# Rewriting a mixer's vector work and order, and starting each SwiGLU stage with three units on the first token half

## The chip, the cores and the metric

The kernel runs on one core of a Trainium2 chip. The metric is the device time of one execution in microseconds (us). Each engine (TensorE for matmuls, VectorE, ScalarE, GpSimd, and SyncE, which issues the DMAs) runs its own instructions in its own fixed order and waits for others by semaphores.

## What is computed

One inference step of a two-layer encoder for 64 sample tokens and 512 prompt tokens, 576 in all, in float32. Per layer, cut to what matters:

```
x = x + 0.5 * post1(SwiGLU_1(pre1(x)))            # w_gate, w_up: 1024 x 2816, w_down: 2816 x 1024
h = pre2(x); z = h @ w_in[l]                      # q_a 384, kv_a 256, kpe 64, hq hf hi hg 256 each, cu cv 256 each
mix = concat[MLA(512) | HGRN2(256) | chunk-gMLP(256)] @ w_out[l]
x = x + post2(mix)
x = x + 0.5 * post3(SwiGLU_2(pre3(x)))
# HGRN2, chunks of 64:  A[t,s] = sum_e q[t,e] k[s,e] exp(b[t,e] - b[s,e]) for s <= t;  o = A v + (q exp b) S
#   o = rmsnorm per head (o, out_g) * silu(hg)
# chunk-gMLP: u = gelu(cu); v = rmsnorm per group (gelu(cv), v_g); out = u * (tril(w_s) v + b_s)
# MLA: c = rmsnorm(kv_a, g) joins the cached latents, the rotary key joins the cached keys; softmax attention
```

All norms are RMS norms over a row. The outputs are y for both groups, and per layer the new latents, rotary keys, HGRN states and gMLP rows.

## The kernel before

**Tiling.** Tokens lie in the free dimension, in two halves of 288 columns (`HALF`); features lie in 8 blocks of 128 partitions. A matmul in float32 is three matmuls of rounded parts (`three`): hi x hi, hi x lo, lo x hi. A weight chunk (`cols`, L121 to L130) is loaded raw by SyncE, then ScalarE writes its rounded part `wh` (L126) and VectorE the remainder `wl` (L127). A unit of gate or up, u, is 8 feature blocks x 3 matmuls for each half.

**Stages.** Six stages run: FFN(0,0), mixer 0, FFN(0,1), FFN(1,0), mixer 1, FFN(1,1), named by layer and place. Each ends by making its update d of the token stream x: per half, `after` spawns `post`, in which the column sum `ss` of squares (an accumulation by L315, then TensorE) gives m (L236), its root p comes from GpSimd (L151) and is spread over partitions by flips (`bc`, transposes on TensorE, L73); then for each feature block d is scaled (L253), added to x (L256) and split into hh and hl (L142); GpSimd sums the squares for the next norm (L198), and `pre_stats` (ss, m L209, root rn, bc) gives the factor `rbc` of the next stage. Here L198 stands for acc, L240 for p.

**FFN.** `ffn` (L327) begins with four weight chunks (`self.ahead`, from `first`, L274): gate and up of the feature blocks f = 0 and 1, prepared while the stage before ends. It runs them on half 0 as soon as x of half 0 is there (`together` waits in the plan for `pre_done`), then on half 1; f = 2 and 3 follow as units on both halves. `evac` (L335 to L341) multiplies by rbc, takes Silu and multiplies. The blocks f = 4 to 21 follow in pairs (`seven`), then `d` by w_down in groups, whose last one ends with three tail blocks half by half.

**Mixer.** `mixer` (L1046) projects by columns of w_in: hq and hf first, then natural rows (tokens in partitions) of hi and hg (vg), cu and cv (uv), then kv_a and kpe in 320 columns (tile n), then three units of q_a (u). Generators run beside it. `hgrn` (L650) makes the decay products: 14 items of a level h and one of two key blocks m. `make` (L695) writes e by two subtractions (L701, L702) and Exp (L703), the product w = k * e on GpSimd (L705), and zb = q * e on VectorE (L711, two per item); `use` multiplies them on TensorE (lv, ls) and copies by a mask (L726, L733). Then come states (su), outputs (o, `out`, L839 and L841), gMLP rows (`cmlp`, L851 to L870) and the normalised latents cn (`latent`, L902), each flipped on TensorE (tp) through one of two small PSUM buffers. `caches` brings the cached latents (ck, cch) and `rotary_key` the rotary key (kd, kp); then v, q, k and the attention.

**What sets the order.** `Net` is a planner: it adds up an estimated TensorE time `self.t` for each matmul, and a spawned generator is stepped when its planned time has come (`spawn`, `tick`, `until`); a `yield` says how long to wait for the next step. `self.pace` (L59) is the planned time between two decay items. The engines' rows are afterwards put in order by a scheduler, by priority and readiness; `keep_in_program_order` pins chosen instructions.

Of the kernel before, what the change touches and what calls it, by code (L numbers as in the profile page):

```python
# [49 lines left out]
class Net:  # L50
    def __init__(self, tc, i, o):
        self.tc = tc
        self.nc = tc.nc
        self.i = i
        self.o = o
        self.count = 0
        self.bg = []
        self.t = 0.0
        self.pace, self.apace, self.l1, self.l2, self.l3 = 3.0, 2.16, 1.26, 3.94, 2.15  # L59

# [266 lines left out]
    def ffn(self, l, j, gpost, gpre, gain, nxt, packed):  # L327
# [14 lines left out]

        chs, self.ahead = self.ahead, None
        for hf in (0, 1):
            o = self.units(chs, hf, 2 if gpost is self.g0 else 4)
            if hf == 0:
                self.until(lambda: 0 in self.stats_done)
                for f in (0, 1):
                    evac(f, 0, o[2 * f][0], o[2 * f + 1][0])
        chs = None  # L350
        ops = self.combine(gain)
        self.until(lambda: 1 in self.stats_done)
        for f in (0, 1):
            evac(f, 1, o[2 * f][1], o[2 * f + 1][1])
        o = None
        for f in (2, 3):
            pg = self.unit(self.cols(wg, f * P))
            pu = self.unit(self.cols(wu, f * P))
            for hf in (0, 1):
                evac(f, hf, pg[hf], pu[hf])  # L360
        for f in range(4, NF, 2):
# [5 lines left out]
        for a, (g0, g1) in enumerate(GROUPS):  # L367
# [36 lines left out]
            if last:  # L404
                chs = [self.cols(wd, m * P, P, g0, g1 - g0) for m in range(tail, KT)]
                self.ahead = [self.cols(*q) for q in nxt]
                for hf in (0, 1):
                    for m in range(tail, KT):
                        run(m, chs[m - tail], [hf])
                    self.after(hf, d, acc, gpost, gpre, (r, r2), packed)  # L410

# [213 lines left out]
    def group_norm(self, src):  # L625
        nc = self.nc
        sq = self.slot("gsq")
        nc.scalar.activation(sq[:, :256], src, AF.Square)
        ss = self.small("gs", 4)
        nc.vector.tensor_reduce(ss, sq[:, :256].rearrange("p (g d) -> p g d", g=4), AX.X, ALU.add)  # L630
        nc.vector.tensor_scalar(ss, ss, 1.0 / 64, EPS, op0=ALU.mult, op1=ALU.add)
        r = self.small("gr", 4)
        self.rsqrt(r, ss, 4)
        return r.unsqueeze(2).to_broadcast([P, 4, 64])

    def to_mix(self, src, k0, i):
        ps = self.sm("tp")
        for e in range(2):
            self.flip(ps[:, e * P:(e + 1) * P], src[:, e * P:(e + 1) * P])
        c, w = tcol(i), twid(i)  # L640
        for e in range(2):
            self.split(self.mixh[k0 + e][:, c:c + w], self.mixl[k0 + e][:, c:c + w], ps[:, e * P:e * P + w])

# [6 lines left out]
    def hgrn(self, l, zq, zf, vg):  # L650
# [36 lines left out]
        for m in range(2):  # L687
            qk.append(self.slot("qk"))
            nc.gpsimd.tensor_tensor(qk[m], q[m], kk[m], op=ALU.mult)
        items = [(li, h, m) for li, h in enumerate(LEVELS) for m in range(2)]  # L690
        ready = {}

        def make(n):
# [18 lines left out]
            ready[n] = (w, z)  # L712

# [59 lines left out]
        for m in range(2):  # L773
            e = self.slot("e")
            nc.vector.tensor_tensor(e[:, :64], b[m][:, 63:64].to_broadcast([P, 64]), b[m][:, :64], op=ALU.subtract)
            bv = b[m][:, 64:].rearrange("p (b x) -> p b x", x=P)
            nc.vector.tensor_tensor(e[:, 64:].rearrange("p (b x) -> p b x", x=P),
                                    bv[:, :, P - 1:P].to_broadcast([P, 4, P]), bv, op=ALU.subtract)
            nc.scalar.activation(e, e, AF.Exp)
            eb[m] = self.slot("eb")  # L780
            nc.scalar.activation(eb[m], b[m], AF.Exp)
            nc.gpsimd.tensor_tensor(e, e, kk[m], op=ALU.mult)
# [18 lines left out]
        for i in (1, 2, 3, 4, 0):  # L801
            for m in range(2):
# [7 lines left out]
                for g in range(2):  # L810
# [8 lines left out]
                yield 0.1  # L819
        while not self.gated:  # L820
# [3 lines left out]
        def out(i):  # L824
# [14 lines left out]
            nc.vector.tensor_tensor(on[:, :256].rearrange("p (g d) -> p g d", g=4),  # L839
                                    ps[:, :256].rearrange("p (g d) -> p g d", g=4), r, op=ALU.mult)  # L840
            nc.vector.tensor_tensor(on[:, :256], on[:, :256], vg[i][:, 256:512], op=ALU.mult)  # L841
            yield 7.71
            self.to_mix(on, 4, i)
            self.left -= 1
# [6 lines left out]
    def cmlp(self, l, i, t, c):  # L851
        nc = self.nc
        v = t[:, 256:512]
        r = self.group_norm(v)
        vv = v.rearrange("p (g d) -> p g d", g=4)
# [21 lines left out]
    def gates(self, l, c, vg, uv):  # L877
# [3 lines left out]
        for i in range(5):  # L881
            nc.scalar.activation(uv[i][:, :512], uv[i][:, :512], AF.Gelu_apprx_tanh)
            self.spawn(self.cmlp(l, i, uv[i], c), 0.8 + 2.59 * i)
        for i in range(5):
            g = vg[i][:, 256:512]
            nc.scalar.activation(g, g, AF.Silu)
            nc.gpsimd.tensor_tensor(g, g, c["og"], op=ALU.mult)
        self.gated = True


    def latent(self, l, i, ps, c, r, kr, cth, ctl):
# [13 lines left out]
        else:  # L905
            nc.sync.dma_start(self.o["ckv_p"][l, 0, (i - 1) * P:i * P], cn[:, :256])
        yield 4.0
        if not cth:
# [137 lines left out]
    def mixer(self, l, gpost, gpre, nxt, packed):  # L1046
# [14 lines left out]

        c["og"] = self.gain_rows("hgrn_out_g", l)
        nch = self.nat_chunks(w, 1216, 512)
# [149 lines left out]
        for k0 in (4, 0):  # L1213
# [29 lines left out]
            if k0 == 0:  # L1243
                for m in range(tail, KT, 2):
                    chs[m // 2] = self.cols(wo, m * P, 2 * P, k0, 4)
                self.ahead = [self.cols(*q) for q in nxt]
                for hf in (0, 1):
                    for m in range(tail, KT):
                        run(m, [hf])
                    self.after(hf, d, acc, gpost, gpre, None, packed)  # L1250

# [33 lines left out]
    def bounds(self, more):  # L1285
        nc = self.nc
        ps = self.sm("tp")
        self.flip(ps[:, :18], more)
        nc.vector.tensor_copy(self.colg[:, 96:], ps[:, :18])

# [18 lines left out]
    def build(self):  # L1309
# [9 lines left out]

        pin = tc.keep_in_program_order  # L1320
        self.ident = load("ident", [P, P])
# [23 lines left out]
        for _ in range(8):  # L1345
            self.mul(self.warm[:, :P], self.ones, self.ones, True, True)
        self.colg = const.tile([P, 114], F32, name="colg", tag="colg")
        ps = self.sm("tp")
# [27 lines left out]
        load_x(4)  # L1376
        self.ahead += [self.cols(*q) for q in todo[2:]]
        more = const.tile([18, P], F32, name="more", tag="more")
        nc.sync.dma_start(more[0:6], i["mla_qa_g"].rearrange("l (k p) -> (l k) p", p=P))
        nc.sync.dma_start(more[6:10], i["hgrn_lb_logits"].rearrange("l (k p) -> (l k) p", p=P))  # L1380
        nc.sync.dma_start(more[10:18], i["cmlp_b_s"].rearrange("l g t -> (l g) t"))
        self.bs = self.colg[:, 106:114]
        self.spawn(self.pre_stats(0, 0.17, sums))
        self.spawn(start(1), 4.06)
# [77 lines left out]
```

## Time and profile before

| | us |
|---|---|
| median of 3 runs | 2287.99 |
| lowest, highest | 2287.04, 2290.99 |
| profiled execution | 2284.6 |
| its span | 2282.8 |
| TensorE busy | 2214.3 (97%) |
| VectorE busy | 1554.9 (68%) |
| ScalarE busy | 1093.4 (48%) |
| GpSimd busy | 225.6 (10%) |

The span runs from the first to the last instruction; the time of the execution has what lies around it as well. Busy time of TensorE counts matmuls at whichever clock was granted. The mixers lie at about 431 to 731 and 1557 to 1860 us; the FFN stages fill the rest.

### The profile page before, as it was taken

Reading aid. Unit: us, or ns where it says so; the run is one execution under the profiler, and the core shown is the slowest. Engines: PE = TensorE matmul, PEld = TensorE weight load, DVE = VectorE, ACT = ScalarE, POOL = GpSimd, SP = SyncE. Lnnn points to the kernel's source line nnn. Section 1 sums busy time; section 2 is a strip of 40 time slices with the busy share of each in tenths; the row PEclk is TensorE's granted clock in tenths of the full one; section 3 lists DMA queues with packets and bytes.
Section 4 is the critical chain, followed back from the end, with each engine's and each line's share of the span. In section 5 each row is a group of like instructions: output and inputs, shape, how many; then the busy total and the mean of one; then the engine's idle time right before and its main releaser. Section 6 shows DMA issues by size and latency. Waiting matters only on the chain.

```text
span 2282.8 us, 39582 instructions
## 1 busy us (share of the span) xinstructions
PE 2214.3 (97%) x15988; PEld 2157.1 (94%) x15988; DVE 1554.9 (68%) x2627; ACT 1093.4 (48%) x1917; POOL 225.6 (10%) x230
## 2 busy tenths in 40 slices
PE   9999999998899999999999999999988999999998
PEld 8999999888799999999999999998887999999998
DVE  6787643787666888845597875447975678887443
ACT  7444442466554644443354444324645645444423
POOL 0000000343301100000020000004332020000000
PEclk9999999999999999999999999999999999999999
DMA  7333442312112333344133334423121232333421
GB/s 218 93 93 93 120 135 84 98 53 78 54 57 79 107 93 93 94 129 125 56 98 93 93 89 133 127 65 102 40 87 48 63 112 72 98 93 101 122 70 42
DMA packets 339531, 211.06 MB, mean 92 GB/s; under 512 B 17378, under 2 KB 319700, under 8 KB 339348
## 3 DMA queue, kind: packets, MB, share of 16 engines
q1 hardware_dynamic: 339348, 208.54, 30.6%
q8 instruction: 125, 2.05, 0.4%
q14 instruction: 58, 0.48, 0.1%
HBM read 190.11 MB, written 18.38 MB: 91 GB/s over the span
## 4 chain that ended last, share of the span: by engine, by line
PE 80%; DVE 10%; ACT 3%; issue 3%; POOL 3%; DMA 0%; SPq 0%; POOLq 0%; DVEq 0%; ACTq 0%
PE d L68 24%; PE X L68 20%; PE Q L68 10%; PE u L68 8%; PE R L68 5%; PE wo L68 4%; DVE zb L711 2%; PE n L68 2%; PE sc L68 1%; DVE x L256 1%; DVE hl L142 1%; DVE d L253 1%; DVE wl L127 1%; PE q L68 1%; PE oT L68 1%
## 5 line engine op out<-in xcount | busy, mean ns | idle before, releaser
L68 PE MATMUL d<-gh,wh 128*128 128x288 f32 x1408 | 413.5, 297 | 2.7 <-ACT gh L138 2.7
L68 PE MATMUL d<-gl,wh 128*128 128x288 f32 x1408 | 413.9, 295 | 0.0
L68 PE MATMUL d<-gh,wl 128*128 128x288 f32 x1408 | 412.7, 294 | 0.0
L127 DVE TENSOR_TENSOR wl<-wr,wh 128x1024 fp32r<-128x1024 f32 (+3 forms) x190 | 224.0, 1183 | 177.7 <-ACT wh L126 176.2
L126 ACT ACTIVATE wh<-wr 128x1024 fp32r<-128x1024 f32 (+3 forms) x190 | 191.5, 1011 | 297.2 <-PE d L68 166.9
L68 PEld LDWEIGHTS d<-gh,wh 128*128 128x128 f32 x1408 | 262.3, 187 | 3.6 <-ACT gh L138 3.6
L68 PEld LDWEIGHTS d<-gh,wl 128*128 128x128 f32 x1408 | 264.8, 188 | 0.0
L68 PEld LDWEIGHTS d<-gl,wh 128*128 128x128 f32 x1408 | 264.1, 188 | 0.0
L68 PE MATMUL X<-th,wh 128*128 128x288 f32 x864 | 255.7, 296 | 0.0
L68 PE MATMUL X<-tl,wh 128*128 128x288 f32 x864 | 254.9, 295 | 0.0
L68 PE MATMUL X<-th,wl 128*128 128x288 f32 x864 | 254.0, 294 | 0.0
L68 PE MATMUL u<-hh,wh 128*128 128x288 f32 x736 | 223.4, 305 | 3.1 <-ACT x L1368 1.5
L138 ACT ACTIVATE wh<-wr 128x1024 fp32r<-128x1024 f32 x144 | 152.1, 1056 | 154.2 <-PE R L68 68.5
L68 PE MATMUL u<-hl,wh 128*128 128x288 f32 x736 | 223.0, 303 | 1.2 <-DVE hl L142 1.2
L68 PE MATMUL u<-hh,wl 128*128 128x288 f32 x736 | 221.7, 302 | 0.0
L139 DVE TENSOR_TENSOR wl<-ws,wh 128x1024 fp32r<-128x1024 f32 x108 | 132.5, 1226 | 100.5 <-ACT wh L138 100.2
L139 DVE TENSOR_TENSOR wl<-wr,wh 128x1024 fp32r<-128x1024 f32 x144 | 175.6, 1222 | 15.8 <-ACT wh L138 14.4
L151 POOL TENSOR_TENSOR p<-m,mhalf 128x3 f32<-128x3 f32 (+1 forms) x14 | 14.4, 1030 | 1713.8 <-DVE m L234 1507.8
L395 DVE TENSOR_TENSOR d<-d,d 128x288 f32<-128x288 f32 x128 | 55.3, 455 | 182.0 <-PE d L68 181.9
L138 ACT ACTIVATE wh<-ws 128x1024 fp32r<-128x1024 f32 x108 | 114.6, 1061 | 132.6 <-DVE ws L502 96.1
L68 PEld LDWEIGHTS X<-th,wl 128*128 128x128 f32 x864 | 162.8, 188 | 0.0
L68 PEld LDWEIGHTS X<-tl,wh 128*128 128x128 f32 x864 | 162.2, 188 | 0.0
(364 smaller groups left out, 5781.8 us busy)
## 6 DMA issues: line engine op xcount, KB each, us to landing
wr<-ffn_w_gate SPq DMA_DIRECT2D x144, 256.0 KB, 3.0
wr<-ffn_w_up SPq DMA_DIRECT2D x144, 256.0 KB, 3.4
wr<-ffn_w_down SPq DMA_DIRECT2D x64, 512.0 KB, 4.2
wr<-w_in SPq DMA_DIRECT2D x30, 512.0 KB, 3.7
xd<-x SPq DMA_DIRECT2D x48, 288.0 KB, 2.4
x<-xd SPq DMA_DIRECT2D x48, 288.0 KB, 5.5
wr<-ffn_w_down SPq DMA_DIRECT2D x32, 384.0 KB, 3.5
wr<-ffn_w_gate SPq DMA_DIRECT2D x16, 512.0 KB, 3.9
```

The source lines that it names most:

```text
L68: self.nc.tensor.matmul(out, lhsT, rhs, start=start, stop=stop, skip_group_check=onto)
L126: nc.scalar.activation(hi[:, :a * b], raw[:, :a * b], AF.Copy)
L127: nc.vector.tensor_tensor(lo[:, :a * b], raw[:, :a * b], hi[:, :a * b].bitcast(F32), op=ALU.subtract)
L138: nc.scalar.activation(hi, src, AF.Copy)
L139: nc.vector.tensor_tensor(lo, src, hi.bitcast(F32), op=ALU.subtract)
L142: nc.vector.scalar_tensor_tensor(lo, src, scale, hi.bitcast(F32), op0=ALU.mult, op1=ALU.subtract)
L151: self.nc.gpsimd.tensor_tensor(out, m, self.mhalf[:, :n], op=ALU.pow)
L253: nc.vector.scalar_tensor_tensor(d[s][:, sl], d[s][:, sl], gpost[s], bc, op0=ALU.mult, op1=ALU.mult)
L256: nc.vector.tensor_tensor(self.x[k][:, sl], self.x[k][:, sl], d[k][:, sl], op=ALU.add)
L395: nc.vector.tensor_tensor(d[m][:, sl], d[m][:, sl], ps[hf][:, :n], op=ALU.add)
L711: nc.vector.tensor_tensor(zo, qv[rs, :, h:], ev[rs, :, h:], op=ALU.mult)
```

## The change

It has two parts. **In the mixer**, products that GpSimd made go to VectorE: q * k (L689), w (now in place in the half of e that is used, so half as wide), the state factor e * k (L782), and the gains of the gated rows and of the output. `out` and `cmlp` multiply by norm and gate in four operations of 64 columns each in place of whole-width ones; the output gain hgrn_out_g becomes a per-partition scale in `to_mix`, so its row DMA goes, and four rows join a load at the start. Exp, Gelu and Silu are pinned in program order on ScalarE. The pace of the decay items becomes 2.2 for 3.0, two yields are longer, and the caches and the rotary key are spawned ahead of the three q_a units. **At an FFN stage**, six chunks in place of four are prepared: half 0 runs three pairs (f = 0, 1, 2), then half 1 the same; only f = 3 is left as a unit. The two more chunks are converted behind the last tail matmuls of the stage before.

```
-        self.pace, ... = 3.0, ...
+        self.pace, ... = 2.2, ...
-        return [(g, 0), (u, 0), (g, P), (u, P)]
+        return [(g, 0), (u, 0), (g, P), (u, P), (g, 2 * P), (u, 2 * P)]
...
         chs, self.ahead = self.ahead, None
+        more = chs[4:] or None
+        chs = chs[:4]
         for hf in (0, 1):
             o = self.units(chs, hf, 2 if gpost is self.g0 else 4)
...
+            if more is None:
+                more = [self.cols(wg, 2 * P), self.cols(wu, 2 * P)]
+            o += self.units(more, hf)
...
+            self.until(lambda: hf in self.stats_done)
+            for f in (0, 1, 2):
+                evac(f, hf, o[2 * f][hf], o[2 * f + 1][hf])
...
-                self.ahead = [self.cols(*q) for q in nxt]
+                self.ahead = [self.cols(*q) for q in nxt[:4]]
                 for hf in (0, 1):
                     for m in range(tail, KT):
                         run(m, chs[m - tail], [hf])
+                    if hf == 1:
+                        chs = None
+                        self.ahead += [self.cols(*q) for q in nxt[4:]]
                     self.after(hf, d, acc, gpost, gpre, (r, r2), packed)
...
-            nc.scalar.activation(e[:, c0:], e[:, c0:], AF.Exp)
-            w = self.slot("w")
-            nc.gpsimd.tensor_tensor(w[:, c0:], kk[m][:, c0:], e[:, c0:], op=ALU.mult)
+            self.pin(nc.scalar.activation(e[:, c0:], e[:, c0:], AF.Exp))
...
+            kv = kk[m][:, c0:].rearrange("p (b x) -> p b x", x=2 * h)
+            nc.vector.tensor_tensor(ev[:, :, :h], ev[:, :, :h], kv[:, :, :h], op=ALU.mult)
+            ready[n] = (e, z)
...
-            nc.vector.tensor_tensor(on[:, :256]..., ps[:, :256]..., r, op=ALU.mult)
-            nc.vector.tensor_tensor(on[:, :256], on[:, :256], vg[i][:, 256:512], op=ALU.mult)
+            for g in range(4):
+                gs = slice(g * 64, (g + 1) * 64)
+                nc.vector.scalar_tensor_tensor(on[:, gs], ps[:, gs], r[:, g:g + 1], vg[i][:, 256 + g * 64:320 + g * 64],
+                                               op0=ALU.mult, op1=ALU.mult)
...
-        nc.vector.tensor_tensor(vv, vv, r, op=ALU.mult)
-        nc.gpsimd.tensor_tensor(v, v, c["vg"], op=ALU.mult)
+        for g in range(4):
+            gs = slice(g * 64, (g + 1) * 64)
+            nc.vector.scalar_tensor_tensor(v[:, gs], v[:, gs], r[:, g:g + 1], c["vg"][:, gs], op0=ALU.mult, op1=ALU.mult)
...
-        c["og"] = self.gain_rows("hgrn_out_g", l)
...
+        lat.append(self.spawn(self.rotary_key(l, kr, a), 6.0))
+        cg = self.spawn(self.caches(l, c), 0.0)
...
-        cg = self.spawn(self.caches(l, c), 0.0)
-        lat.append(self.spawn(self.rotary_key(l, kr, a), 1.0))
```

The other hunks: the yields 0.1 to 0.6 in the state loop and 4.0 to 8.0 in `latent`; `group_norm` returns the plain column; the same `nxt[:4]`, `nxt[4:]` split in the mixer's tail (L1243 to L1250); the pins on the other Exp, on Gelu and on Silu.

**TensorE, first mixer, the last decay items.** n is the 320-column projection, lv and ls the products of an item, tp<-cn the flip of a latent tile, su a state product, u a q_a unit. Before, the first flip of cn:

```order
L68 MATMUL lv_5644<-zb_5007,w_5537 128x128 x4
L68 MATMUL ls_5651<-zb_5007,w_5537 64x64
L68 MATMUL n_5625<-wh_5566,hh_4657 128x320
L68 MATMUL n_5625<-wl_5567,hh_4657 128x320
L68 MATMUL n_5625<-wh_5566,hl_4658 128x320
L68 MATMUL n_5625<-wh_5566,hh_4688 128x320
L68 MATMUL n_5625<-wl_5567,hh_4688 128x320
L68 MATMUL n_5625<-wh_5566,hl_4689 128x320
L73 MATMUL tp_5664<-ident_c,cn_5622 128x128 x2
L68 MATMUL n_5682<-wh_5554,hh_4502 128x320
```

In the changed kernel the first two flips of cn:

```order
L68 MATMUL n_5873<-wh_5583,hh_4628 128x320
L68 MATMUL n_5873<-wl_5584,hh_4628 128x320
L68 MATMUL n_5873<-wh_5583,hl_4629 128x320
L73 MATMUL tp_5785<-ident_c,cn_5646 128x128 x2
L68 MATMUL su_5798<-vg_5065,kdn_5707 128x128
L68 MATMUL n_5873<-wh_5589,hh_4658 128x320
L68 MATMUL n_5873<-wl_5590,hh_4658 128x320
L68 MATMUL n_5873<-wh_5589,hl_4659 128x320
L68 MATMUL n_5873<-wh_5589,hh_4689 128x320
L68 MATMUL n_5873<-wl_5590,hh_4689 128x320
```

The first flip stood between the last two items, in front of the matmuls of tile n_5682; now it stands behind all items, six matmuls before the end of the projection's last tile, n_5873.

**TensorE, first mixer, the caches and the rotary key.** ck is the cached latents' tile, kd the rotary key's; v are values, q queries. Before:

```order
L73 MATMUL tp_6374<-ident_c,on_6257 128x128 x2
L68 MATMUL ss_6479<-ones,accq_5848 128x1 x6
L73 MATMUL tp_6573<-ident_c,ck_6437 128x128
L73 MATMUL tp_6504<-ident_c,kd_6445 128x128 x3
L68 MATMUL v_6538<-wh_6399,cth_5660 128x512
L68 MATMUL v_6538<-wl_6400,cth_5660 128x512
L68 MATMUL v_6538<-wh_6399,ctl_5662 128x512
L68 MATMUL v_6538<-wh_6399,cth_5661 128x512
```

In the changed kernel:

```order
L73 MATMUL tp_6190<-ident_c,cn_5979 128x128 x2
L73 MATMUL tp_6197<-ident_c,oc_6025 128x128 x2
L73 MATMUL tp_6232<-ident_c,kd_6129 128x128 x3
L73 MATMUL tp_6206<-ident_c,ck_6003 128x128 x4
L73 MATMUL tp_6254<-ident_c,kd_6130 128x128 x2
L68 MATMUL u_6306<-hh_4503,wh_6302 128x288
L68 MATMUL u_6306<-hl_4504,wh_6302 128x288
```

The flips stood behind the queries, among the values that read them; now they stand ahead of the third q_a unit.

**VectorE, the end of mixer 0 and start of FFN(0,1).** L315 sums squares of d, L236 (m) opens half 1's chain, L127 converts a weight chunk. Before:

```order
L142 SCALAR_TENSOR_TENSOR hl_8070<-x_7694,colg,hh_8069 128x288
L1236 TENSOR_TENSOR d_7670<-d_7670,wo_8054 128x288
L253 SCALAR_TENSOR_TENSOR d_7670<-d_7670,colg,bc_7962 128x288
L256 TENSOR_TENSOR x_7696<-x_7696,d_7627 128x288
L315 TENSOR_TENSOR acc_1269_7689<-acc_1269_7689,sq_8077 128x288
L142 SCALAR_TENSOR_TENSOR hl_8070<-x_7695,colg,hh_8069 128x288
L236 TENSOR_SCALAR m_8107<-ss_8103 128x3
L256 TENSOR_TENSOR x_7697<-x_7697,d_7670 128x288
L142 SCALAR_TENSOR_TENSOR hl_8125<-x_7696,colg,hh_8124 128x288
L127 TENSOR_TENSOR wl_8489<-wr_8486,wh_8488 128x1024
```

In the changed kernel:

```order
L1241 TENSOR_TENSOR d_7670<-d_7670,wo_8054 128x288
L127 TENSOR_TENSOR wl_8083<-wr_8080,wh_8082 128x1024
L315 TENSOR_TENSOR acc_1254_7689<-acc_1254_7689,sq_8077 128x288
L127 TENSOR_TENSOR wl_8089<-wr_8086,wh_8088 128x1024
L253 SCALAR_TENSOR_TENSOR d_7670<-d_7670,colg,bc_7962 128x288
L256 TENSOR_TENSOR x_7696<-x_7696,d_7627 128x288
L142 SCALAR_TENSOR_TENSOR hl_8070<-x_7695,colg,hh_8069 128x288
L236 TENSOR_SCALAR m_8119<-ss_8115 128x3
L256 TENSOR_TENSOR x_7697<-x_7697,d_7670 128x288
L142 SCALAR_TENSOR_TENSOR hl_8137<-x_7696,colg,hh_8136 128x288
L127 TENSOR_TENSOR wl_8608<-wr_8605,wh_8607 128x1024
```

Two conversions now stand around the last L315, ahead of m; the one behind m was there before. (L1241 is the former L1236; the change shifts later lines by some five.)

## Rows read from the trace of the kernel before

**Rows 1.** Page, section 1: busy us of each engine, share of the span, instructions.
```profile
PE 2214.3 (97%) x15988; PEld 2157.1 (94%) x15988; DVE 1554.9 (68%) x2627; ACT 1093.4 (48%) x1917; POOL 225.6 (10%) x230
```

**Rows 2.** Waits of TensorE, first mixer (421 to 632 us): us, times, longest.
```profile
PE tp L73 <- DVE cn L902: 4.5, 1, 4.5
...
PE v L68 <- ACT cch L138: 2.0, 1, 2.0
PE tp L73 <- DVE kd L932: 1.5, 1, 1.5
...
PE tp L73 <- DMA ck<-cache_mla_ckv: 0.6, 1, 0.6
```

**Rows 3.** Waits of TensorE, second mixer (1545 to 1760 us).
```profile
PE tp L73 <- DVE cn L902: 3.9, 1, 3.9
PE lv L68 <- DVE zb L711: 2.3, 1, 2.3
PE v L68 <- ACT cch L138: 2.2, 1, 2.2
...
PE tp L73 <- DVE kd L932: 1.6, 1, 1.6
...
PE k L68 <- ACT v L1166: 0.9, 1, 0.9
PE q L68 <- ACT v L1166: 0.9, 1, 0.9
```

**Rows 4.** Windows: length, busy us (records) of PE, PEld, DVE, ACT, POOL; PEclk, DMA, GB/s.
```profile
537.30:544.10 6.80, 5.62 (x23) 5.63 (x24) 3.06 (x10) 1.10 (x5) 0.81 (x2) 0.50 0.34 110
...
sum 37.40, PE 31.91 PEld 28.75 DVE 18.96 ACT 17.23 POOL 5.45; mean PE 4.56 PEld 4.11 DVE 2.71 ACT 2.46 POOL 0.78
...
545.00:605.00 60.00, 54.29 (x397) 50.23 (x396) 43.00 (x136) 27.54 (x76) 26.88 (x29) 1.00 0.28 85
```

**Rows 5.** Waits of TensorE as FFN stages start: (0,1), (1,0), (0,0).
```profile
PE ss L68 <- POOL acc L198: 1.7, 1, 1.7
...
PE bc L73 <- POOL p L151: 0.6, 1, 0.6
...
PE bc L73 <- POOL rn L151: 1.9, 1, 1.9
PE ss L68 <- DVE acc L315: 1.7, 1, 1.7
PE bc L73 <- DVE p L240: 1.1, 1, 1.1
...
PE u L68 <- ACT x L1368: 0.9, 1, 0.9
```

**Rows 6.** Windows, 495 to 525 us: the lv records alone, then the n records.
```profile
495.00:525.00 30.00, 6.31 (x48) 6.27 (x48) 4.57 (x12) 1.00 0.06 16
...
495.00:525.00 30.00, 23.11 (x96) 17.37 (x97) 0.00 (x0) 2.69 (x4) 1.00 0.06 16
```

**Rows 7.** Groups by line and form, levels (480 to 545, L705 440 to 640): busy, mean ns, idle before.
```profile
L711 DVE TENSOR_TENSOR zb<-z,e 64x288 f32<-64x288 f32 x24 | 23.0, 960 | 4.7 <-ACT e L703 4.5
...
L701 DVE TENSOR_TENSOR e<-b 128x288 f32<-128x288 f32 x11 | 5.5, 502 | 0.2
...
L705 POOL TENSOR_TENSOR w<-k,e 128x576 f32<-128x576 f32 x12 | 19.4, 1620 | 30.3 <-ACT e L703 24.2 <-PE ls L68 6.1
```

**Rows 8.** Groups of VectorE by line and form, 545 to 610 us.
```profile
L870 DVE SCALAR_TENSOR_TENSOR oc<-cm,colg,uv 128x64 f32<-128x64 f32 x16 | 3.5, 277 | 0.5 <-PE cm L68 0.5
...
L839 DVE TENSOR_TENSOR on<-o,gr 128x256 f32<-128x256 f32 x5 | 2.1, 425 | 5.4 <-POOL gr L151 5.4
```

**Rows 9.** Windows of TensorE in FFN(0,0): length, busy us (records), clock, DMA, GB/s.
```profile
330.00:340.00 10.00, 10.00 (x78) 1.00 0.74 242
```

**Rows 10.** Timeline of VectorE, 735 to 765 us: start, us, engine, line, operation.
```profile
739.55 1.22 DVE L127 TENSOR_TENSOR wl<-wr,wh 128x1024 fp32r<-128x1024 f32 x1
```

**Rows 11.** Timeline of TensorE, 755 to 758 us; in brackets idle before and releaser.
```profile
756.93 0.83 PE L68 MATMUL ss<-ones,acc 128*128 128x1 f32 x6 [1.70 <-POOL acc L198]
```

More of the change, by code (lines that the diff above doesn't have):

```diff
@@ L58, in __init__ @@
         self.t = 0.0
-        self.pace, self.apace, self.l1, self.l2, self.l3 = 3.0, 2.16, 1.26, 3.94, 2.15
+        self.pace, self.apace, self.l1, self.l2, self.l3 = 2.2, 2.16, 1.26, 3.94, 2.15
     def mul(self, out, lhsT, rhs, start, stop, onto=False):
@@ L343, in ffn @@
         chs, self.ahead = self.ahead, None
+        more = chs[4:] or None
+        chs = chs[:4]
         for hf in (0, 1):
             o = self.units(chs, hf, 2 if gpost is self.g0 else 4)
[L346 to L360, printed above, removed]
+            if hf == 1:
[3 more added lines that the diff above has]
+            o += self.units(more, hf)
+            if hf == 1:
+                more = None
+                ops = self.combine(gain)
+            self.until(lambda: hf in self.stats_done)
+            for f in (0, 1, 2):
+                evac(f, hf, o[2 * f][hf], o[2 * f + 1][hf])
+            o = None
+        pg = self.unit(self.cols(wg, 3 * P))
+        pu = self.unit(self.cols(wu, 3 * P))
+        for hf in (0, 1):
+            evac(3, hf, pg[hf], pu[hf])
         for f in range(4, NF, 2):
@@ L409, in ffn @@
                         run(m, chs[m - tail], [hf])
+                    if hf == 1:
+                        chs = None
+                        self.ahead += [self.cols(*q) for q in nxt[4:]]
                     self.after(hf, d, acc, gpost, gpre, (r, r2), packed)
@@ L633, in group_norm, with to_mix @@
         self.rsqrt(r, ss, 4)
-        return r.unsqueeze(2).to_broadcast([P, 4, 64])
-    def to_mix(self, src, k0, i):
+        return r
+    def to_mix(self, src, k0, i, scale=(None, None)):
         ps = self.sm("tp")
@@ L641, in to_mix @@
         for e in range(2):
-            self.split(self.mixh[k0 + e][:, c:c + w], self.mixl[k0 + e][:, c:c + w], ps[:, e * P:e * P + w])
+            self.split(self.mixh[k0 + e][:, c:c + w], self.mixl[k0 + e][:, c:c + w], ps[:, e * P:e * P + w], scale=scale[e])
     def mix_rows(self, ks):
@@ L688, in hgrn @@
             qk.append(self.slot("qk"))
-            nc.gpsimd.tensor_tensor(qk[m], q[m], kk[m], op=ALU.mult)
+            nc.vector.tensor_tensor(qk[m], q[m], kk[m], op=ALU.mult)
         items = [(li, h, m) for li, h in enumerate(LEVELS) for m in range(2)]
@@ L778, in hgrn @@
                                     bv[:, :, P - 1:P].to_broadcast([P, 4, P]), bv, op=ALU.subtract)
-            nc.scalar.activation(e, e, AF.Exp)
+            self.pin(nc.scalar.activation(e, e, AF.Exp))
             eb[m] = self.slot("eb")
-            nc.scalar.activation(eb[m], b[m], AF.Exp)
-            nc.gpsimd.tensor_tensor(e, e, kk[m], op=ALU.mult)
+            self.pin(nc.scalar.activation(eb[m], b[m], AF.Exp))
+            nc.vector.tensor_tensor(e, e, kk[m], op=ALU.mult)
             qe[m] = self.slot("qe")
@@ L838, in out @@
             on = self.slot("on")
-            nc.vector.tensor_tensor(on[:, :256].rearrange("p (g d) -> p g d", g=4),
-                                    ps[:, :256].rearrange("p (g d) -> p g d", g=4), r, op=ALU.mult)
-            nc.vector.tensor_tensor(on[:, :256], on[:, :256], vg[i][:, 256:512], op=ALU.mult)
+            for g in range(4):
+                gs = slice(g * 64, (g + 1) * 64)
+                nc.vector.scalar_tensor_tensor(on[:, gs], ps[:, gs], r[:, g:g + 1], vg[i][:, 256 + g * 64:320 + g * 64],
+                                               op0=ALU.mult, op1=ALU.mult)
             yield 7.71
-            self.to_mix(on, 4, i)
+            self.to_mix(on, 4, i, [self.og[:, 2 * l + e:2 * l + e + 1] for e in range(2)])
             self.left -= 1
@@ L885, in gates @@
             g = vg[i][:, 256:512]
-            nc.scalar.activation(g, g, AF.Silu)
-            nc.gpsimd.tensor_tensor(g, g, c["og"], op=ALU.mult)
+            self.pin(nc.scalar.activation(g, g, AF.Silu))
         self.gated = True
@@ L1245, in mixer @@
                     chs[m // 2] = self.cols(wo, m * P, 2 * P, k0, 4)
-                self.ahead = [self.cols(*q) for q in nxt]
+                self.ahead = [self.cols(*q) for q in nxt[:4]]
                 for hf in (0, 1):
@@ L1249, in mixer @@
                         run(m, [hf])
+                    if hf == 1:
+                        chs.clear()
+                        self.ahead += [self.cols(*q) for q in nxt[4:]]
                     self.after(hf, d, acc, gpost, gpre, None, packed)
@@ L1287, in bounds @@
         ps = self.sm("tp")
-        self.flip(ps[:, :18], more)
-        nc.vector.tensor_copy(self.colg[:, 96:], ps[:, :18])
+        self.flip(ps[:, :22], more)
+        nc.vector.tensor_copy(self.colg[:, 96:], ps[:, :22])
         L = self.colg[:, 102:106]
@@ L1376, in build @@
         load_x(4)
-        self.ahead += [self.cols(*q) for q in todo[2:]]
-        more = const.tile([18, P], F32, name="more", tag="more")
+        self.ahead += [self.cols(*q) for q in todo[2:4]]
+        more = const.tile([22, P], F32, name="more", tag="more")
         nc.sync.dma_start(more[0:6], i["mla_qa_g"].rearrange("l (k p) -> (l k) p", p=P))
@@ L1381, in build @@
         nc.sync.dma_start(more[10:18], i["cmlp_b_s"].rearrange("l g t -> (l g) t"))
+        nc.sync.dma_start(more[18:22], i["hgrn_out_g"].rearrange("l (k p) -> (l k) p", p=P))
         self.bs = self.colg[:, 106:114]
+        self.og = self.colg[:, 114:118]
         self.spawn(self.pre_stats(0, 0.17, sums))
```

12 lines of the change are left out of this document (5 added, 7 removed).

## The prediction

> **What bounds the kernel now.** The page comes first: TensorE is busy for 2214.3 of 2282.8 us [rows 1], so no edit can give back more than the 68.5 us in which it stands still, and what it loses in stretches at half clock. The next view is that of the waits of TensorE, by stretch, since a wait names the engine that was late. In the first mixer the change touches four long ones: 4.5 us for cn (the latent's normalised rows, VectorE), 2.0 for the cached latents (ScalarE's copy cch), 1.5 for the rotary key kd, and 0.6 for the cache's DMA [rows 2]. The second repeats them, adds 2.3 us for zb, the scaled queries of a decay level, and 0.9 and 0.9 for v behind the caches [rows 3]. Third come the windows of the stretches in which the granted clock is 0.50, the lower of the two levels (1.2 instead of 2.4 GHz): seven in the mixers, 37.4 us with 31.91 us of work in them [rows 4]. Work at half rate takes twice as long, so these cost at most 31.91 / 2 = 16.0 us. Most begin at or just behind one of the long waits, the first at 537.3 us around the wait for cn. Fourth are the starts of the three later FFN stages, where TensorE waits for the update of the token stream: 0.6 and 1.7 us in FFN(0,1), 1.1, 1.7 and 1.9 in FFN(1,0) [rows 5]; FFN(1,1) repeats FFN(0,1) to within 0.1.
>
> **The levels of the decay product.** An item (a level and one of two key blocks; 14 in a layer) is made by VectorE, ScalarE and GpSimd and used by TensorE, with n matmuls of the projection laid between by the planner. Six items take 30 us: 48 records of lv (8 for an item) and 96 of n, 16 for an item [rows 6]. TensorE is full there, so the levels themselves cost nothing that VectorE could give back. VectorE needs two L711 of 0.960, L701 and its mirror L702, and the copies; L711 is long because GpSimd runs the product w (L705, 1.62 us) beside it: L701, also 288 elements a lane, takes 0.502 [rows 7]. The change moves w to VectorE at half width, one more 0.50, and takes 2 x (0.96 - 0.50) = 0.92 away: about 0.4 us less of VectorE per item, and no 1.62 us on GpSimd in the chain. With a pace of 2.2 for 3.0 the order puts 12 n between items for 15. At 23.11 / 96 = 0.24 us each, an item lasts 0.7 us less on TensorE, VectorE still keeps up, and the 14 items end some 10 us sooner. No work goes: the n that were between the items now stand behind them, and that is where the gain is. All 120 matmuls of the 320-column projection are left when the last item is done, and the order puts the first flip of cn behind 114 of them, no longer between the last two items. I take both waits for cn as gone: 4.5 + 3.9 = **-8.4**. Of the 2.3 for zb in layer 1, where q and k products now share VectorE, I take half: **-1.2** (bounds 0 and -2.3).
>
> **Caches and rotary key moved.** They are now spawned ahead of the three query units and the order puts their flips before unit 2, so that values and queries no longer stand behind them. The waits that go are 2.0 + 1.5 + 0.6 and 2.2 + 1.6 + 0.9 + 0.9 = **-9.7** [rows 2, 3]. Their five or six copies and rotary products on VectorE must then fit earlier, which is the next term.
>
> **The new dense place.** The flips of cn, the state products su, cm, the outputs o and the flips of kd and ck now stand close together on TensorE with hardly a matmul between, and each needs one of two small PSUM buffers back from VectorE or ScalarE. In the same part of before VectorE was busy 43.00 of 60 us [rows 4], so there is room on the mean, but not at each place. The vector work added there is bounded by rows: two TT of 0.42 become four of 0.277 (L870 is the nearest, the same 128x64 operation) [rows 8], +0.27 for each of five outputs; for the gated rows one TT of 0.42 and a product on GpSimd become four of 0.277, +0.68 for five: 4.7 us in a mixer at most. Against it GpSimd is free of its products, and the group norms' square roots, which queue there, come sooner. So from 0 to 4.7 in each mixer; I take 2 in each, since 17 of 60 us were free: **+4**. ScalarE, with Exp, Gelu and Silu kept in order, loses table loads (43 in the order, then 17); ScalarE ends none of these waits alone, so I price that at nothing.
>
> The Trainium skill (Perfetto Trace Analysis, Optimizing Scalar/DVE Operations) says that each vector operation pays about 60 ns on SBUF and 125 ns on PSUM whatever its size, and that larger operations help once the engine is saturated, which speaks against cutting one operation in four. An estimate by these figures, 0.2 us for each of ten places, makes it about 2 us in a mixer and the term +4, where the rows allow up to +9.4. The engine is not saturated on the mean in that stretch by the row just named.
>
> **Half clock in the mixers.** Six of the seven stretches lie at waits that go; the seventh comes behind the wait for zb and may stay. Of the 16.0 us I take back six tenths, since new short waits can keep some: **-9.5** (bounds -3 and -16).
>
> **The start of an FFN stage.** Two more weight pairs (gate and up of f = 2) are now converted before the stage, so that half 0 has 144 matmuls in place of 96 before half 1 is needed. In full-clock stretches 78 matmuls of 288 columns end in 10 us [rows 9], 0.128 each: 48 are 6.1 us of cover. But the stage's work is the same in sum, and VectorE is full there: the order puts both conversions around the last square sum L315 and ahead of m, the step that opens half 1's chain; before, they stood behind it. One takes 1.22 us [rows 10], so the chain is 2.4 us late. In FFN(0,1) TensorE waits 1.7 us in front of half 1's sum ss, until 756.93 [rows 11]; with the delay that is 759.3. Before, 140 u matmuls preceded it, now 144: TensorE arrives 0.5 us later. The wait grows by 1.9, and with what the one for p may add or spare I take **+2.0**. FFN(1,1) is alike, **+2.0**. In FFN(1,0) more u's now cover the wait for p, but 12 fewer stand between p and rn, so the 1.9 us grow by the 1.5 that these took: **+1.5**. A wait of 4 us at one place is as long as the one for cn, which has 6.8 us at half clock around it with 5.62 of work [rows 4], 2.8 us lost; I count two thirds of one, **+2.0**. FFN(0,0) has its f = 2 units ready in place of the 0.9 us wait at x [rows 5]: **-0.9**.
>
> **The rest.** A DMA of a gain row goes and four more rows come in a load at the start; the scale in the flips' evacuation turns two copies into scaled ones of the same length. Nothing waits for either.
>
> **Sum.** -8.4 - 1.2 - 9.7 + 4 - 9.5 = -24.8 in the mixers; 2.0 + 2.0 + 1.5 + 2.0 - 0.9 = +6.6 at the FFN starts: -18.2. The profiled execution took 2284.6 us, 1.8 more than its span; that gives 2266.4. The median of the three runs shown lies 3.4 above it: **2269.8, say 2270**. With the terms at their bounds this case spans 2260 to 2279.
>
> **Rivals.**
> - *The FFN starts gain after all.* If the chain of half 1 isn't what is late (VectorE's conversions fall into its own waits), the 48 matmuls cover the waits of 0.6, 1.7, 1.1, 1.7 and 1.9 instead: no +6.6, and some 5 us less. 2270 - 12 = 2258. For it speaks that 6.1 us of cover is more than any of these waits; against it that VectorE's timeline has hardly a hole there.
> - *The mixers' waits only move.* VectorE becomes the bound of the dense place: each cn flip that no longer waits in the projection waits among su and o. Then only -9.7 and half of the clock (-4.7) stay, against +9.4 and +6.6: +1.6, 2286 on the profiled run, 2290 as a median. It decides where VectorE's 43 us of 60 come to more than 50.
> - *Slower: the conversions cost at each step of the chain.* If the 2.4 us come before p, before rn and before ss, each of the three later starts pays up to 7.2, and 2.8 for the clock: 3 x 10.0 = +30, with the mixers at their upper bound of the dense place (-19.4) and FFN(0,0)'s -0.9: +9.7, which gives 2298. It decides once a start's waits together pass about 10 us.
> - *The change doesn't do what it says.* The order shows the moved rows, but TensorE's rows can move while VectorE's queue, not the pace, says when items are ready; then the time stays at 2284 to 2291.
>
> **How the numbers follow.** Chances: the forecast 0.52, the FFN gain 0.16, the moved waits 0.15, slower 0.11, no effect 0.06. A measurement of this kernel can tell about 0.2%, 4.6 us, from no change. Faster: 0.52 + 0.16 and a third of the moved waits, 0.73; the same 0.16; slower 0.11. The range reaches from 2256, inside the first rival, to 2290, which takes in the moved waits and leaves the slower case out.
>
> **What would show it.** In the changed kernel no wait for cn, cch or kd over 0.5 us and no half clock around the end of the levels; a cluster of waits of 0.3 to 1 us on flips and o some 10 us behind them, 2 us more than before; in front of half 1's ss a single wait of 3 to 4 us in FFN(0,1) and FFN(1,1), with half clock behind it. The prediction is wrong if the mixers together save under 12 us, or if the three starts save anything.

## The result: slower, and the profile after

The changed kernel takes 2309.22 us (median; 2306.72 to 2310.75) beside 2287.98 before: a ratio of 1.0094, 95% interval 1.0082 to 1.0106, 21 us slower. The forecast was 2270, the range 2256 to 2290: the sign is wrong. Cut at the first matmul of each stage, the two traces give these lengths; idle and half clock are TensorE's within the stage, in us. (Mixer 0 so cut begins at 416.75 us and mixer 1 at 1540.78, earlier than the section on the profile before puts them.)

| stage | before | after | difference | idle before, after | half clock before, after |
|---|---|---|---|---|---|
| FFN(0,0) | 416.75 | 417.56 | +0.8 | 6.1, 6.7 | 10.2, 10.2 |
| mixer 0 | 314.56 | 324.20 | +9.6 | 19.0, 21.7 | 20.5, 41.0 |
| FFN(0,1) | 403.77 | 408.32 | +4.6 | 4.3, 6.4 | 0, 6.8 |
| FFN(1,0) | 405.70 | 406.99 | +1.3 | 5.4, 6.5 | 3.4, 3.4 |
| mixer 1 | 318.83 | 322.97 | +4.1 | 22.0, 18.8 | 23.9, 44.4 |
| FFN(1,1) | 423.22 | 423.97 | +0.8 | 4.4, 6.5 | 11.5, 12.4 |

The FFN stages lose 7.4 us, as forecast (+6.6). The mixers lose 13.8 where 24.8 were to be won, and not by waiting more: their idle time is 0.5 us less in sum, but 41 us more of them pass at half clock. Each column is one execution, and a single stage can differ by some 3 us without cause in its code: FFN(1,0), unchanged in e4 and e6 below, took 409.1 us in the profiles of both, with 10.2 at half clock.

The page's first section, to be read against [rows 1]: TensorE is busy 15.6 us longer with the same number of matmuls, so they ran slower.

```profile
PE 2229.9 (97%) x15988; PEld 2169.3 (94%) x15988; DVE 1537.3 (67%) x2713; ACT 1059.8 (46%) x1891; POOL 149.4 (6%) x174
```

Waits of TensorE in the changed kernel's first mixer (421 to 640 us; total, times, longest). Against [rows 2] the flips' wait for cn and that for the cache's DMA are gone and kd's is shorter, but k now waits 2.8 us for ScalarE where v waited 2.0, and a row of new waits for VectorE among cm, u, o and su has come (one of them, 1.1 us, is o's for a row of cn).

```profile
PE k L68 <- ACT v L1171: 2.8, 1, 2.8
PE tp L73 <- DVE ml L139: 2.2, 2, 1.7
...
PE u L68 <- DVE on L847: 2.0, 1, 2.0
PE cm L68 <- DVE ctl L139: 1.5, 1, 1.5
PE cm L68 <- DVE st L821: 1.4, 1, 1.4
PE o L68 <- DVE cn L908: 1.1, 1, 1.1
...
PE tp L73 <- DVE kd L938: 1.0, 1, 1.0
PE q L68 <- ACT v L1171: 0.9, 1, 0.9
```

Windows on these dense places (columns as in [rows 4]): 27.3 and 30.7 us in one piece at clock 0.50, where the longest piece in a mixer before was 6.8 us.

```profile
571.30:598.60 27.30, 18.09 (x73) 15.07 (x74) 17.68 (x77) 6.21 (x25) 5.89 (x6) 0.50 0.23 61
1707.90:1738.60 30.70, 23.81 (x100) 20.54 (x99) 19.74 (x85) 6.11 (x25) 6.57 (x7) 0.50 0.16 44
```

Some 25 us ahead of the first piece, ScalarE's timeline has this: Gelu and Silu, kept in order, stand in one block with their two table loads, and the square gsq of the group norm comes behind it. VectorE's timeline shows who pays (7.4 us in mixer 1).

```profile
540.50 1.28 ACT L889 ACT_TABLE_LOAD   x1
541.79 2.72 ACT L889 ACTIVATE uv<-uv 128x512 f32<-128x512 f32 x5
544.51 1.28 ACT L893 ACT_TABLE_LOAD   x1
545.80 1.65 ACT L893 ACTIVATE vg<-vg 128x256 f32<-128x256 f32 x5
547.36 0.40 ACT L634 ACTIVATE gsq<-uv 128x256 f32<-128x256 f32 x1
```

```profile
547.79 0.42 DVE L636 TENSOR_REDUCE gs<-gsq 128x4 f32<-128x256 f32 x1 [7.14 <-ACT gsq L634]
```

At the start of FFN(0,1), VectorE's timeline has the two conversions and then m; TensorE's has the wait in front of half 1's ss, 4.10 us for 1.70 in [rows 11].

```profile
746.65 1.22 DVE L127 TENSOR_TENSOR wl<-wr,wh 128x1024 fp32r<-128x1024 f32 x1
747.79 0.45 DVE L315 TENSOR_TENSOR acc<-acc,sq 128x288 f32<-128x288 f32 x1
748.16 1.22 DVE L127 TENSOR_TENSOR wl<-wr,wh 128x1024 fp32r<-128x1024 f32 x1
...
751.26 0.15 DVE L236 TENSOR_SCALAR m<-ss 128x3 f32<-128x3 f32 x1
```

```profile
769.49 1.23 PE L68 MATMUL ss<-ones,acc 128*128 128x1 f32 x5 [4.10 <-POOL acc L198]
```

### The profile page after: what moved, and what is told of

Its sections match the earlier page's. It is cut to its first block, busy times and chain, and to the rows that moved or that the text cites. A ratio compares the mean times of both kernels' runs of the same rounds, so it can differ in the third digit from the quotient of the medians.

```text
span 2304.0 us, 39529 instructions
## 1 busy us (share of the span) xinstructions
PE 2229.9 (97%) x15988; PEld 2169.3 (94%) x15988; DVE 1537.3 (67%) x2713; ACT 1059.8 (46%) x1891; POOL 149.4 (6%) x174
## 4 chain that ended last, share of the span: by engine, by line
PE 85%; DVE 7%; ACT 3%; POOL 2%; issue 1%; DMA 1%; SPq 0%; POOLq 0%; DVEq 0%; ACTq 0%
PE d L68 24%; PE X L68 20%; PE Q L68 10%; PE u L68 9%; PE n L68 5%; PE R L68 5%; PE wo L68 4%; PE sc L68 1%; DVE x L256 1%; DVE hl L142 1%; PE lv L68 1%; DVE d L253 1%; PE q L68 1%; PE oT L68 1%; POOL acc L198 1%
## 5 line engine op out<-in xcount | busy, mean ns | idle before, releaser
L127 DVE TENSOR_TENSOR wl<-wr,wh 128x1024 fp32r<-128x1024 f32 (+3 forms) x190 | 220.6, 1164 | 184.4 <-ACT wh L126 183.4
L68 PEld LDWEIGHTS X<-th,wh 128*128 128x128 f32 x864 | 161.9, 187 | 0.0
```

The source lines that it names most:

```text
L68: self.nc.tensor.matmul(out, lhsT, rhs, start=start, stop=stop, skip_group_check=onto)
L127: nc.vector.tensor_tensor(lo[:, :a * b], raw[:, :a * b], hi[:, :a * b].bitcast(F32), op=ALU.subtract)
```

## The experiments

Ratios are to the kernel before, with their 95% interval; it ran again beside each group of experiments, with medians from 2285.47 to 2287.70 us, so between groups the ratios are the safer comparison. "The vector work" is all the mixer's hunks but the pace, the two yields and the place of caches and rotary key.

**The four parts, e1 to e4.** e1 has the hunks of `first`, `ffn` and the two stage tails alone; e2 all the others; e3 the vector work alone; e4 the mixer's order alone.

> Only the FFN part of the change: three pairs of gate and up on half 0, two more chunks converted ahead of the stage; the mixer as in the kernel before. If the stage lengths add up (FFN stages of the changed kernel +0.8, +4.6, +1.3 and +0.8 us against before), this kernel is 7 to 8 us slower than before, about 2295, with one wait of about 4 us in front of half 1's ss in FFN(0,1) and FFN(1,1). If the FFN stages of the changed kernel were late only because its mixers hand over late, it is within 2 us of before.

> Only the mixer part (vector work and order), FFN stages as before. If the parts add up: +9.6 and +4.1 us in the mixers, 2302, with half clock for 27 to 31 us in the dense place of each mixer. If the two parts disturb each other, the sum with e1 misses 21 us by more than 3.

> Mixer's vector work alone (products from GpSimd to VectorE, four operations of 64 columns, output gain as a scale, Exp, Gelu and Silu pinned), pace 3.0, yields and the place of caches and rotary key as before. Theory of the place (the moved order empties the dense place of long matmuls, which brings half clock): 2282 to 2289, no stretch of half clock over 10 us in a mixer. Rival, theory of the vector work (VectorE, given more operations, is late in the dense place): 2296 to 2302, with waits of 1 to 2 us for VectorE among su, cm and o as in the changed kernel.

> Mixer's order alone: pace 2.2, longer yields, caches and rotary key ahead of the q_a units; vector work as before. Theory of the place: 2298 to 2306, with a stretch of over 20 us at half clock in each mixer. Rival, theory of the vector work: 2282 to 2292, waits in the dense place not longer than before.

| | median us | ratio |
|---|---|---|
| e1 | 2294.12 | 1.0029 (1.0019 to 1.0039) |
| e2 | 2302.59 | 1.0062 (1.0047 to 1.0077) |
| e3 | 2296.74 | 1.0040 (1.0026 to 1.0055) |
| e4 | 2296.49 | 1.0041 (1.0026 to 1.0056) |

The two parts of the change add (6.6 + 14.2 = 21 us by the ratios, for 21). Both halves of the mixer part cost; e3 came out in its rival's range and e4 between its two, so neither theory was enough. In sum e3 and e4 lose 19 us where e2 loses 14: these two do not simply add. e4's dense places show no long half clock (6.8 us at most), and what its moved rows lose by there isn't worked out; e3's do (23.9 and 27.3 us), behind a wait of VectorE that e4 doesn't have:

```profile
DVE gs L630 <- ACT gsq L628: 7.0, 1, 7.0
```

That pointed at the block on ScalarE.

**Free Gelu and Silu (e5, e6), the pace (e7), late chunks (e8).** e5 is e2 and e6 is e3 with the first edit (and the like one for Silu), e7 is e2 with the second, e8 is e1 with the third; a stage then loads the two chunks itself.

```diff
-            self.pin(nc.scalar.activation(uv[i][:, :512], uv[i][:, :512], AF.Gelu_apprx_tanh))
+            nc.scalar.activation(uv[i][:, :512], uv[i][:, :512], AF.Gelu_apprx_tanh)
...
-        self.pace, ... = 2.2, ...
+        self.pace, ... = 3.0, ...
...
-        return [(g, 0), (u, 0), (g, P), (u, P), (g, 2 * P), (u, 2 * P)]
+        return [(g, 0), (u, 0), (g, P), (u, P)]
```

> The mixer part as in e2, but Gelu and Silu of the gates not kept in program order. Theory of the block (kept in order, ten activations and two table loads stand in one piece of 7 us on ScalarE ahead of the squares that the group norms need, VectorE stands still for 7.1 us there, and the dense place starts late and without cover): 8 to 14 us faster than e2, 2288 to 2295, no wait of VectorE for gsq over 2 us, half clock in the dense place halved or gone. Rival (the dense place falls to half clock because the moved order took its long matmuls away): within 3 us of e2, 2299 to 2306.

> The vector work as in e3, but Gelu and Silu not kept in order. Theory of the block: 8 to 14 us faster than e3, 2283 to 2289, equal to before or a little faster. Rival (the operations moved from GpSimd and the cut in four are what makes VectorE late): within 3 us of e3, 2294 to 2300.

> The mixer part as in e2 with the pace of the decay items at 3.0, as before. Theory of the block: the items' pace is not the cause, 2298 to 2304. Rival (a pace of 2.2 ends the items early and leaves nothing for the dense place): 2289 to 2296 and half clock in the dense place under 15 us.

> The FFN part as in e1, but the two more chunks are loaded and converted as the stage begins, not ahead of it, so that no stage's last steps have them on VectorE. Theory of the queue (two conversions ahead of m delay half 1's chain by 2.3 us): 2284 to 2289, the wait in front of half 1's ss back at 1.7 us or less. Rival (three pairs on half 0 spend the matmuls that used to cover half 1's chain): 2292 to 2296, the wait still at 3.5 us or more.

| | median us | ratio | against its base |
|---|---|---|---|
| e5 | 2289.05 | 1.0011 (1.0001 to 1.0021) | -13.5 |
| e6 | 2282.97 | 0.9978 (0.9963 to 0.9993) | -13.8 |
| e7 | 2307.66 | 1.0085 (1.0069 to 1.0101) | +5.1 |
| e8 | 2284.88 | 0.9993 (0.9981 to 1.0006) | -9.2 |

(The last column is of medians; by the ratios it is -11.7, -14.2, +5.3 and -8.2.) The block is worth 12 to 14 us, twice over. VectorE's waits for gsq, 14.3 us in sum over both mixers of e2 and 14.0 in e3, are 1.0 in e5 and none in e6, although ScalarE loads its tables 37 to 41 times instead of 17. From e2 to e5 the dense places' half clock falls from 58 to 34 us; by the two profiles the mixers are 12.6 us shorter, 5.1 of it less idle time of TensorE and 7.5 the same matmuls run faster: the block costs by the wait and by the clock. With the gates free the vector work is a small gain. e7 missed both its ranges; it speaks against the pace as a cause, since a pace of 3.0 is no better (5 us worse, with intervals that overlap). e8 confirms the queue: the wait in front of ss is down to 0.3 us, and what is left at FFN(0,1) is a wait for the late conversion itself (waits of TensorE, 730 to 765 us):

```profile
PE u L68 <- DVE wl L127: 2.1, 1, 2.1
...
PE ss L68 <- DVE acc L315: 0.3, 1, 0.3
```

**Both mended (e9), both gains (e10), the block alone (e11), the caches alone (e12).** e9 is the changed kernel with the edits of e5 and e8; e10 is e6 with the FFN part as in e8; e11 is the kernel before with its Gelu kept in order; e12 is e6 with this:

```diff
+        lat.append(self.spawn(self.rotary_key(l, kr, a), 6.0))
+        cg = self.spawn(self.caches(l, c), 0.0)
...
-        cg = self.spawn(self.caches(l, c), 0.0)
-        lat.append(self.spawn(self.rotary_key(l, kr, a), 1.0))
```

> The whole change with the two causes found taken out: Gelu and Silu not kept in order (minus 13.5 us between e2 and e5), the two more chunks converted as the stage begins (minus 9 between e1 and e8). If both act alone, 2309 - 13.5 - 9 = 2284 to 2290. If one of them hid the other, 2292 or more.

> The vector work with free Gelu and Silu (e6) and three pairs on half 0 with late chunks (e8), the mixer's order as before. If the gains add (minus 3.0 and minus 1.1), 2280 to 2283, faster than before by 0.1 to 0.3%. If they are only scatter, 2284 to 2288.

> The kernel before with one edit: the five Gelu of a mixer kept in program order. They then stand in one block of a table load and five activations (4.0 us of the 7) ahead of the first gsq. Theory of the block: 4 to 9 us slower than before, 2290 to 2295, and VectorE waits 3 to 4 us for gsq. Rival (the block hurts only beside the new vector work): within 2.5 us of before.

> e6 with the caches and the rotary key spawned ahead of the q_a units, as in the change; pace and yields as before. The prediction's term (their waits of 4 to 5 us in each mixer go): 5 to 9 us faster than e6, 2274 to 2278. Rival (the flips go into the dense place and take the q_a matmuls that covered it): no faster than e6, 2282 to 2290, with half clock over 15 us in the dense place.

| | median us | ratio |
|---|---|---|
| e9 | 2286.52 | 1.0001 (0.9991 to 1.0010) |
| e10 | 2282.03 | 0.9977 (0.9962 to 0.9991) |
| e11 | 2312.74 | 1.0116 (1.0100 to 1.0132) |
| e12 | 2295.29 | 1.0034 (1.0021 to 1.0047) |

e9 lands where the sum put it: two edits take back the 21 us against the kernel before. They don't explain the 39 us against the forecast: e9 still carries the caches' place, which costs 12 us (e12, e18), and the gains of vector work and pace pay for it. e10's late chunks add nothing to e6 that its ratio shows. e11 shows that a block hurts in the old kernel too, but by 25 us where 4 to 9 were expected, outside both its ranges: VectorE's wait for gsq is the 4.0 us foreseen in each mixer, and o now waits 5.0 and 4.9 us for VectorE's ml where it waited 0.5. TensorE idles 12 us more in the mixers, and its matmuls take as much longer, with 48 us at half clock in mixer 1 alone; why so long there stays open. So keeping Gelu in order can cost more than the wait for gsq. e12 is 12 us slower than e6, against my term of -9.7 and beyond the rival's range too. Its mixers idle 4 us less than e6's, and lose by the clock. Windows of equal length in its dense place and at the like place of the kernel before:

```profile
573.70:601.00 27.30, 25.06 (x112) 23.09 (x111) 15.78 (x66) 4.79 (x18) 6.57 (x6) 0.50 0.16 48
```

```profile
571.70:599.00 27.30, 25.13 (x182) 22.68 (x182) 18.67 (x61) 7.95 (x24) 11.96 (x11) 1.00 0.17 50
```

TensorE is busy for 25 of 27.3 us in both, with 112 matmuls at half clock and 182 at full. In e12, 94 of the 112 are the short ones of su, o, cm and flips (64 and 128 columns), and the 18 q_a matmuls of 288 columns come behind them, in the last 5 us; in the other window 72 of q_a and 12 of v (512 columns) lie in the same stretch.

**Filling the place (e13, e14, e16) and the pace on e6 (e15).** e13 is e12, e14 the changed kernel, e16 e10 with this filling, which writes into the buffer that the real matmuls then write over; e15 is e6 with the pace 2.2:

```diff
             ps = self.mm("o")
+            fh = self.hpart(0, 0)[0]
+            for _ in range(8):
+                self.nc.tensor.matmul(ps[:, :W2], fh[:, :P], fh, start=True, stop=True, skip_group_check=True)
...
         ps = self.sm("cm")
+        fh = self.hpart(0, 0)[0]
+        for _ in range(6):
+            self.nc.tensor.matmul(ps[:, :W2], fh[:, :P], fh, start=True, stop=True, skip_group_check=True)
```

> e12 with 70 matmuls of 288 columns more in each mixer, 8 ahead of each output o and 6 ahead of each cm, whose results are written over: 9.3 us of work for nothing in each mixer at full clock. Theory of the clock (the dense place is slow because a run of short matmuls alone lets the clock fall, and at half rate every link of its chain is longer): no stretch over 7 us at half clock there, and in spite of 19 us of extra work no more than 4 us slower than e12, 2285 to 2299. Rival (VectorE's chain sets the dense place's length, half clock goes along): the extra work adds to what PE does behind it, 2305 to 2314.

> The changed kernel with the same 70 matmuls in each mixer. Theory of the clock: 2300 to 2312, half clock in the dense places under 10 us instead of 27 and 31. Rival (VectorE's chain): half clock may go, but the time rises to 2315 to 2328.

> e6 with the pace of the decay items at 2.2. If the pace, beside the caches, empties the dense place: 4 to 10 us slower than e6, 2287 to 2293, with more half clock there. If the moved caches do it alone: within 3 us of e6, 2280 to 2286.

> e10, the fastest so far, with the same 70 matmuls. Its dense places have 10 and 7 us at half clock. If these are worth their extra work: 2276 to 2284. If not, the work adds: 2288 to 2300.

| | median us | ratio |
|---|---|---|
| e13 | 2285.40 | 0.9999 (0.9988 to 1.0010) |
| e14 | 2312.55 | 1.0118 (1.0100 to 1.0136) |
| e15 | 2278.06 | 0.9963 (0.9950 to 0.9976) |
| e16 | 2283.02 | 0.9984 (0.9974 to 0.9995) |

e13 does 140 matmuls for nothing and is faster than e12 by 8 us (ratios; 10 by the medians). Its dense place runs at full clock:

```profile
570.00:597.00 27.00, 25.02 (x193) 22.93 (x192) 20.16 (x79) 6.58 (x21) 5.94 (x5) 1.00 0.18 50
```

So in e12 the half clock is the loss and not its companion, with one reservation: the filling also moved other rows of the dense place (su and q_a on TensorE, some 20 places on VectorE), and that share isn't tested apart. e14, between its two ranges, doesn't tell the clock from VectorE's chain in the changed kernel. Its filling cuts the half clock there from 58 to 24 us, and the time rises by 3 (medians) to 5 us (ratios); so these 34 us gave back some 15 of the 19 us of extra work, a little under half a microsecond each, and the 55 us in e13 about half each (19 and 8 to 10). That VectorE, 7 us late behind the block, sets the rest of the length is argued, not shown. e16 gains nothing on e10. e15 is faster than both its ranges: against e6 it gives the pace a gain of 5 us by the medians, 3 by the ratios, with intervals that overlap.

**The parts that gain (e17), and the yields (e18).** e17 is the vector work with free gates, pace 2.2, three pairs on half 0 with late chunks; e18 adds the yields 0.6 and 8.0.

> All parts that gained alone: the vector work with free Gelu and Silu, pace 2.2, three pairs on half 0 with late chunks; caches, rotary key and yields as before. If the gains add (e15 at minus 9, late chunks minus 1): 2274 to 2279. If pace and late chunks disturb each other: 2280 to 2288.

> e17 with the two longer yields of the change (states 0.6, latents 8.0), so that it differs from the mended change e9 by the place of the caches and the rotary key alone. If the moved caches are the whole rest of the loss: within 3 us of e17, 2274 to 2281. If the yields have a share: 2281 to 2288.

e17 takes 2275.77 us, ratio 0.9955 (0.9941 to 0.9969); e18 2274.94, ratio 0.9953 (0.9940 to 0.9966). Both beat the kernel before by 10 us and the changed one by 32 (ratios). The yields make no difference. e18 differs from e9 by the place of caches and rotary key alone: 11.6 us, like the 12.3 between e6 and e12. e17 differs from e10 by the pace alone: 5 us by the ratios, the third such pair that points the same way.

## Why the prediction was wrong, step by step

- **ScalarE, priced at nothing: the first step that failed.** I counted table loads saved and did not ask what is queued behind the kept order; that ScalarE "ends none of these waits alone" sits badly with [rows 2], where v waits 2.0 us for its cch. Ten activations and two loads, 7 us, stood ahead of gsq, for which VectorE and then the whole dense place wait: +13.5 by the medians.
- **Caches and rotary key, -9.7: failed, +12.** The waits for ck went and those for kd fell to 1.0 us in each mixer; in place of v's for cch k now waits, 2.8 us. I priced the waits and not what the moved work would stand beside.
- **Half clock in the mixers, -9.5: wrong sign.** In sum it rose from 44 to 85 us (the seven stretches counted, 37.4 us, left out two at the mixers' starts). This is how the two costs above arise in large part, and does not come on top of them. I let the clock follow the waits; in e12 it was at half for 27.3 us with 2.2 of idle time, where the q_a matmuls were gone, and at full again in e13 with others in their place. My step "with hardly a matmul between" named the place and drew only waits from it.
- **The dense place, +4.** Its waits come to some 12 us in mixer 0, and its price is not the four operations per row: on VectorE's timeline four of 64 columns take 0.86 us together for an output, as long as the two of 0.42 they replace, and 0.87 for a gated row, where one of 0.43 and GpSimd's 0.73 went. Four times 0.277 would be 1.11; on the timeline they overlap.
- **The levels, -8.4 and -1.2: right as a mechanism, about half as a gain.** L711 fell from 0.960 to 0.450 us once GpSimd's product was gone, the flips' waits for cn and the one for zb went, the items end 15 us sooner in mixer 0 (10 forecast). Alone, the pace gains some 3 to 6 us in each of three pairs (e7 to e2, e6 to e15, e10 to e17). In the changed kernel the waits moved: the mixers' idle time is the same in sum.
- **FFN starts, +6.6: right, 7.4** (e1: 7.7 by medians). The single wait of 4.1 us in front of ss and its 6.8 us of half clock came where they were put in FFN(0,1), and e8 shows the cause. Off were FFN(1,1), +0.8 for +2.0, where the wait is 4.1 us too but the half clock had been before, and FFN(0,0), +0.8 for -0.9: its wait of 0.9 us stayed.
- **The rivals.** The one on the slower side put the loss into the FFN chain at 2298; the chain cost what the forecast had. "The mixers' waits only move" was right about the waits, though not by its sign: VectorE was busy for 35.56 of 50.50 us there (549.5 to 600), no more of the time than the 43 of 60 before. It stopped at 2290, since neither it nor any other rival named the block on ScalarE or a half clock without waits.
- **The range.** The terms at their own bounds give 2258 to 2283, not 2260 to 2279. Neither holds 2309. By the prediction's own sign, mixers that save under 12 us, it was wrong.

## What to carry to other kernels

Instructions kept in program order are a block for the engine's queue: before pinning, list what stands behind the block and who waits for it; 26 table loads saved here were not worth a wait of 7 us in each mixer. When a wait is moved, look at what the moved instructions then stand between: here a run of short matmuls that lost its long ones cost 12 us, by the clock and not by waits. And work that is prepared ahead for a stage belongs behind the chain that opens the stage, not in front of it on the same engine.

## What the runs showed of the hardware

- TensorE can be at half clock while it is busy: 25.06 of 27.3 us by the profile in e12's dense place, 94 of 112 matmuls with 64 or 128 columns, at granted clock 0.50 throughout. 140 matmuls of 288 columns that compute nothing (70 in each mixer) brought the full clock back there and made the kernel 8 to 10 us faster. The Trainium skill (TensorE: Matmul & The Clock Gate, Part 1: The HAM clock gate) ties the clock to how busy the array has been of late; here the busy time in the windows did not tell the two cases apart (25.06 and 25.13 us), only the granted clock did.
- A product on GpSimd more than doubled the time of a VectorE operation beside it: L711 took 0.960 us on the mean with L705 on GpSimd [rows 7]. Of its 24 records in the kernel before's first mixer, the 18 that ran beside a GpSimd operation for most of their time took 1.13 us on the mean, the 5 that ran without one 0.455. In the changed kernel the same operation (now L715) takes 0.450, and the product (L717) 0.462. The Trainium skill (Perfetto Trace Analysis, Optimizing Scalar/DVE Operations) says that the two share a read port and that moving work between them might not help; the first half fits these rows; as to the second, here VectorE took the product over, and these three operations of an item take it 1.36 us where two took 1.92.

Groups of VectorE by line and form in the changed kernel, 480 to 545 us (busy, mean ns, idle before):

```profile
L715 DVE TENSOR_TENSOR zb<-z,e 64x288 f32<-64x288 f32 x24 | 10.8, 450 | 0.9 <-ACT e L709 0.7
...
L717 DVE TENSOR_TENSOR e<-e,k 128x288 f32<-128x288 f32 x12 | 5.5, 462 | 0.2
```
